# Attention with queries on partitions: scores once, the two maps of a differential head mixed into one, weights turned by TensorE transposes

## The chip, the cores and the metric

The kernel runs on one core of one Trainium2 chip. The core has a TensorE (PE in the profile; its weight loads are a row of their own, PEld), VectorE (DVE), ScalarE (ACT), GpSimd (POOL) and SyncE (SP, which here only issues DMAs). Each engine executes its instructions in the order in which they were built. The metric is the device time of one execution in microseconds; lower is better. All data are fp32. Matrices go through TensorE either as fp32, or as pairs (hi, lo) of fp32r numbers whose sum is the fp32 number, in several passes.

## What is computed

Two layers of a backbone run for 128 prompt tokens and 512 sample tokens (with 2 columns of zeros between them, 642 columns). Each layer is a mixer (differential attention, grouped-query attention, an SSD scan, an S5 scan, one output projection) and a gated ConvFFN. The change is in the two attentions. Sample tokens see their own 512 keys and 128 cached ones, prompt tokens see the prompt's 128 keys alone:

```python
def diff_attention(q, k, v, lam):
    scale = A_HALF ** -0.5
    k1, k2 = k[..., :A_HALF], k[..., A_HALF:]
    def block(qb):
        s1 = jnp.einsum('bqhd,bkhd->bhqk', qb[..., :A_HALF], k1).astype(F32) * scale
        s2 = jnp.einsum('bqhd,bkhd->bhqk', qb[..., A_HALF:], k2).astype(F32) * scale
        p = jax.nn.softmax(s1, axis=-1) - lam * jax.nn.softmax(s2, axis=-1)
        return jnp.einsum('bhqk,bkhd->bqhd', p.astype(v.dtype), v)
...
def gqa_attention(q, k, v):
...
        s = jnp.einsum('bqkgd,bskd->bkgqs', qg, k).astype(F32) * scale
        p = jax.nn.softmax(s, axis=-1)
        o = jnp.einsum('bkgqs,bskd->bqkgd', p.astype(v.dtype), v)
```

There are four differential heads of 64 features (two maps of 32 features each) and four grouped-query heads of 64 features, each two of which share a key head. The differential output is then normed per head.

## The kernel before

**Stages.** In the mixer the queries and keys come from the input projection (`lin3`: three passes over hi and lo parts, PSUM banks `psp`), are normed and rotated in `qk_prep`, split into hi and lo, and stored to DRAM as bands (`d_aq`, `d_ak`, `d_bq`, `d_bk`), from which attention loads them in the layout it wants. The S5 scan goes first; SSD, attention, the rest of the projections and, in layer 0, adaLN's products for later (`wm`, `sc`) then share the engines. A scheduler fixes the order of each engine when the kernel is built, by priorities (`PR`: S5 0, SSD 30000, attention 35000, projections 40000, the filling adaLN products 60000; the lower goes first among what is ready in its own model) and by the buffers that are free. SP issues all loads in one order as well.

**PSUM.** Eight banks: two for big tiles or `psp`, two of `e`, one each of `v` and `u`, two of `d`; `pss` (L157) hands them out. `e` and `u` serve attention's scores, `v` its output, `d` the SSD.

**Attention.** `attention` (L1314) runs six units: for each key half the differential heads' first maps, their second maps, and a grouped-query pair. A unit is two score maps, and `attn_unit` (L1119) gives it four parts. `load` brings cached keys (`ck`, L1135 or L1162), queries and keys (L1142 to L1171). `maxs` computes the scores with queries on the partitions (128 queries by 512 keys in bank `e`), takes row maxima on DVE (L1191; cached keys L1196), and turns them by small matmuls into a row that stands as an extra feature of the queries, with a row of ones on the keys' side (L1212). `probs` computes the scores again with keys on the partitions, the maximum now subtracted by that extra feature, exponentiates on ACT (`at_e`, L1237) and multiplies the values by these: weights of 64 columns (one head's values) and 512 moving columns (queries), in fp32 (`psv<-at_e,vt`). The exponentials are added over the key tiles on DVE and POOL (`at_s`, L1243), summed by a matmul with ones, and inverted by a reciprocal over 512 columns (L1254). `tail` divides, subtracts the second map's result from the first's, norms the head and splits the result for the output projection. The parts of three successive units are woven: `maxs` of unit u+1, `probs` of u, `tail` of u-1.

## Time and profile before

| | |
|---|---|
| device time, median of three runs | 2274.74 us (2268.22 to 2276.24) |
| span of the profiled execution | 2270.7 us |
| mean granted TensorE clock in it | 0.930 of full |
| PE busy | 2064.1 us (91%) |
| DVE, ACT, POOL busy | 1166.1, 728.5, 706.0 us |
| instructions | 32188 |

Busy times are sums of instruction lengths where they don't overlap; an engine at 91% over the whole span may still stand idle in a stage. The chain that ended last is followed back from the last instruction, each step to what released it. Windows give the same sums for stretches, with the granted clock as a share of full speed. Names are `out<-in`; L12 is line 12 of the kernel. A matmul's length overlaps the next one's, so what one holds of the engine is read from start to start.

### The profile page before, as it was taken

What the parts mean: (1) busy time and instruction counts of PE and PEld (TensorE: products, weight loads), DVE (VectorE), ACT (ScalarE), POOL (GpSimd) and SP (SyncE); (2) the same over time, 40 slices, a digit from 0 to 9 for tenths busy, and PEclk for the clock granted to TensorE, in tenths of its full rate; (3) what the DMA queues carried; (4) which work ended last, traced back from release to release, by engine and by line L of the source; (5) the groups of instructions that cost most, each with busy time, mean ns of one, the idle gap of its engine ahead of it and who ended that gap; (6) DMA issues with size and microseconds to landing.
All of it is one profiled execution on the core that took longest, in us unless ns stands there. A gap on an engine that the chain in (4) does not pass through costs nothing.

```text
span 2270.7 us, 32188 instructions
## 1 busy us (share of the span) xinstructions
PE 2064.1 (91%) x12698; PEld 1692.5 (75%) x12698; DVE 1166.1 (51%) x2376; ACT 728.5 (32%) x1256; POOL 706.0 (31%) x747
## 2 busy tenths in 40 slices
PE   5994988899999999999988889887989999999997
PEld 2884753454779788899976877655557899999985
DVE  7864874434558567233335358564565451323343
ACT  3421342232344223223324224343234443323231
POOL 4642523222232344122223324322233231212131
PEclk9996988889999999999998989888988999999998
DMA  7554324314313575422222542321022012222221
GB/s 285 165 179 135 121 68 124 93 49 142 108 38 108 166 247 186 131 82 63 84 77 77 174 131 90 111 67 49 11 65 94 19 47 84 70 80 68 82 75 47
DMA packets 95199, 232.19 MB, mean 102 GB/s; under 512 B 18120, under 2 KB 31816, under 8 KB 95048
## 3 DMA queue, kind: packets, MB, share of 16 engines
q1 hardware_dynamic: 95048, 230.14, 32.0%
q8 instruction: 100, 1.64, 0.3%
q14 instruction: 51, 0.42, 0.1%
HBM read 193.52 MB, written 36.58 MB: 101 GB/s over the span
## 4 chain that ended last, share of the span: by engine, by line
PE 75%; DMA 9%; DVE 7%; POOL 3%; issue 2%; ACT 2%; SPq 2%; POOLq 0%; DVEq 0%; ACTq 0%
PE psb L85 34%; PE psp L85 14%; PE pse L85 9%; PE psv L85 7%; PE psd L85 7%; PE psu L85 2%; DMA wm<-in_w_mod 1%; DMA ck<-in_cache_bk 1%; DMA ck<-in_cache_ak 1%; DMA wr<-in_w_down 1%; DMA s5yd<-s_u 1%; DMA wr<-in_w_out 1%; DMA s_tb<-s5td 1%; DMA s_u<-s5ud 1%; SPq L1160 1%
## 5 line engine op out<-in xcount | busy, mean ns | idle before, releaser
L85 PE MATMUL psb<-hh,wh 128*128 128x256 f32 (+1 forms) x1152 | 358.9, 312 | 2.3 <-DVE cv L425 2.3
L85 PE MATMUL psb<-hl,wh 128*128 128x256 f32 (+1 forms) x1152 | 357.9, 311 | 0.0
L85 PE MATMUL psb<-hh,wl 128*128 128x256 f32 (+1 forms) x1152 | 357.0, 310 | 0.0
L106 POOL TENSOR_TENSOR wl<-wr,wh 128x1024 fp32r<-128x1024 f32 (+3 forms) x83 | 181.6, 2188 | 449.5 <-ACT wh L103 427.1
L103 ACT CAST wh<-wr 128x1024 fp32r<-128x1024 f32 (+3 forms) x166 | 160.4, 966 | 427.9 <-PE psb L85 285.1
L85 PEld LDWEIGHTS psb<-hh,wh 128*128 128x128 f32 x1152 | 217.8, 189 | 13.2 <-issue 8.2
L85 PEld LDWEIGHTS psb<-hl,wh 128*128 128x128 f32 x1152 | 218.5, 190 | 3.4 <-issue 3.4
L85 PEld LDWEIGHTS psb<-hh,wl 128*128 128x128 f32 x1152 | 217.8, 189 | 3.4 <-issue 3.4
L85 PE MATMUL psp<-hh,wh 128*128 128x386 f32 (+1 forms) x544 | 182.2, 335 | 40.2 <-DVE dtr L839 13.1
L106 DVE TENSOR_TENSOR wl<-wr,wh 128x1024 fp32r<-128x1024 f32 (+3 forms) x83 | 95.2, 1147 | 184.5 <-ACT wh L103 184.0
L85 PE MATMUL psp<-hl,wh 128*128 128x386 f32 (+1 forms) x544 | 176.3, 324 | 1.5 <-DVE hl L353 1.4
L85 PE MATMUL psp<-hh,wl 128*128 128x256 f32 (+1 forms) x544 | 175.6, 324 | 0.0
L85 PE MATMUL psb<-uh,wh 128*128 128x256 f32 (+1 forms) x544 | 169.7, 312 | 0.0
L85 PE MATMUL psb<-ul,wh 128*128 128x256 f32 (+1 forms) x544 | 168.9, 310 | 0.0
L85 PE MATMUL psb<-uh,wl 128*128 128x256 f32 (+1 forms) x544 | 168.6, 310 | 0.0
L85 PEld LDWEIGHTS psp<-hh,wh 128*128 128x128 f32 x544 | 109.7, 202 | 52.8 <-DVE dtr L839 13.6
L85 PE MATMUL psv<-at_e,vt 128*64 128x512 f32 x240 | 136.3, 681 | 10.2 <-ACT at_e L1237 10.1
L1377 POOL TENSOR_TENSOR cv<-cv,cv 128x642 f32<-128x642 f32 x44 | 71.3, 1622 | 169.6 <-DVE cv L425 140.2
L85 PE MATMUL pse<-k,q 96*128 96x128 f32 (+5 forms) x288 | 100.2, 407 | 21.9 <-issue 6.7
L424 DVE SCALAR_TENSOR_TENSOR cv<-psb,vec,cv 128x641 f32<-128x641 f32 x72 | 63.4, 881 | 103.3 <-ACT cv L423 103.3
L85 PEld LDWEIGHTS pse<-k,q 96*128 96x128 f32 (+2 forms) x288 | 54.4, 205 | 79.0 <-issue 59.6
L85 PEld LDWEIGHTS psp<-hl,wh 128*128 128x128 f32 x544 | 109.5, 201 | 4.0 <-DVE hl L353 2.5
(497 smaller groups left out, 4596.5 us busy)
## 6 DMA issues: line engine op xcount, KB each, us to landing
wm<-in_w_mod SPq DMA_DIRECT2D x96, 512.0 KB
wr<-in_w_up SPq DMA_DIRECT2D x88, 512.0 KB
wr<-in_w_in SPq DMA_DIRECT2D x30, 512.0 KB
wr<-in_w_down SPq DMA_DIRECT2D x32, 384.0 KB
wr<-in_w_down SPq DMA_DIRECT2D x32, 320.0 KB
wr<-in_w_out SPq DMA_DIRECT2D x16, 512.0 KB
s_tb<-s5td SPq DMA_DIRECT2D x8, 992.0 KB
s_to<-s5td SPq DMA_DIRECT2D x8, 768.0 KB
```

Of the source, the lines that this page charges most:

```text
L85: self.nc.tensor.matmul(out, w, x, start=start, stop=stop)
L103: nc.scalar.copy(hv, rv)
L106: e.tensor_sub(lv, rv, hv.bitcast(F32))
L424: nc.vector.scalar_tensor_tensor(out[:, 1:TW], x[:, 0:TW - 1], w[:, 0:1], out[:, 1:TW], op0=ALU.mult, op1=ALU.add)
L1160: nc.sync.dma_start(k2[0:64, 0:TW].bitcast(F32), self.qd["bk"][0, r])
L1377: G.tensor_mul(cv[0], cv[0], cv[1])
```

## The change

Queries now stay on the partitions all the way. A unit of kind 0 is one differential head with both its maps; a unit of kind 1 is a pair of grouped-query heads as before. A unit is a list of items, the prompt and four tiles of 128 queries for each head, each with a `front` and a `back`; with `LAG = 1` the front of an item comes before the back of the one ahead of it.

`front` computes the scores of 128 queries with 512 keys into a bank of `e` (those of the cached keys for several tiles into `u`), takes the maximum on DVE, combines it with that of the cached keys and scales it in a small DVE step (L1252), and exponentiates on ACT with this as a bias for each partition; ACT sums the row as it goes (`accum_out`). For a differential head, `mix` adds the second map, times -lam and the ratio of the two sums, to the first: one operation on 128x640. `back` turns the weights by transposes on TensorE, four tiles of 128x128 into a bank of `e` (L1184), splits them into hi (ACT) and lo (DVE, L163), and multiplies: the turned weights are now the stationary operand, the values (as hi and lo side by side, `vhl`) move, 128 columns for hi and 64 for lo. The output has queries on its partitions, so division and head norm take a number for each partition; last it is turned back (L1293). The loads of a unit are issued before the items of the unit ahead of it, from two `k` buffers and four `q` buffers (before three and six), with `d_bk` as three bands and `d_bq` as two.

```diff
-KB = 3
+KB = 2
-QN = 6
-DEL = (4, 0, 0)
-STEP = (1, 1, 1)
-RSP = 1
+QN = 4
+LAG = 1
+NP = 4
-AB = ("e", "u", "e", "e", "u", "ue")
...
         lo = pool.tile([P, TW], F32R, tag="qk_lo", name="qk_lo")
         self.split(hi, lo, R)
-        n = 2 if name == "bk" else 3
+        n = 2 if name[:2] == "bq" else 3
...
-    def attn_unit(self, l, pool, kq, kind, u, aa=0):
+    def attn_unit(self, l, pool, kq, kind, u, m0=0):
...
+        if kind == 0:
+            c, hi = cached(256)
+            cv, hv = (t.rearrange("p (m k) -> p m k", m=2) for t in (c, hi))
+            nc.sync.dma_start(cv[0:96], self.a["cache_ak"][l, u, :, 2 * m0:2 * m0 + 2, :])
+            A.copy(kt_[0:64, :, CK], cv[0:64])
+            A.copy(hv[64:96], cv[64:96])
+            V.tensor_sub(kt_[64:96, :, CK], cv[64:96], hv[64:96].bitcast(F32))
+            for i in range(2):
+                f = 32 * (2 * m0 + i)
+                nc.sync.dma_start(q[i][0:96].bitcast(F32), self.qd[f"aq{u}"][:, f:f + 32])
+                nc.sync.dma_start(kt_[0:96, i, 0:TW].bitcast(F32), self.qd[f"ak{u}"][:, f:f + 32])
+            def score(out, i, qs, ks):
+                self.mm(out, q[i][0:96, qs], kt_[0:96, i, ks], True, True)
+        else:
+            k1, k2 = kt_[:, 0, :], kt_[:, 1, :]
+            r = slice(64 * u, 64 * u + 64)
+            nc.sync.dma_start(k1[:, 0:TW].bitcast(F32), self.qd["bk"][0:2, r])
+            nc.sync.dma_start(k2[0:64, 0:TW].bitcast(F32), self.qd["bk"][2, r])
+            c, _ = cached(128)
+            nc.sync.dma_start(c, self.a["cache_bk"][l, u])
+            A.copy(k1[:, CK], c)
+            V.tensor_sub(k2[0:64, CK], c[0:64], k1[0:64, CK].bitcast(F32))
+            for i in range(2):
+                r = slice(64 * i, 64 * i + 64)
+                nc.sync.dma_start(q[i].bitcast(F32), self.qd[f"bq{u}"][0:2, r])
+            def score(out, i, qs, ks):
+                self.mm(out, q[i][:, qs], k1[:, ks], True, False)
+                self.mm(out, q[i][0:64, qs], k2[0:64, ks], False, True)
+        vhl = kq.tile([P, 6, 128], F32R, tag="v", name="v", bufs=2)
+        c = 64 * (2 * u + m0 if kind == 0 else 4 + u)
+        v = self.vt[:, :, c:c + 64]
+        A.copy(vhl[:, :, 0:64], v)
+        G.tensor_sub(vhl[:, :, 64:128], v, vhl[:, :, 0:64].bitcast(F32))
+        def probs(i, ps, nb, p, z):
+            A.activation(p, ps, AF.Exp, bias=nb, scale=scale, accum_out=z)
+        def mix(p1, p2, z, rz):
+            t = z[:, 2:4]
+            V.reciprocal(t, z[:, 0:2])
+            V.tensor_copy(rz, t[:, 0:1])
+            V.scalar_tensor_tensor(t[:, 1:2], z[:, 0:1], self.nlam, t[:, 1:2], op0=ALU.mult, op1=ALU.mult)
+            V.scalar_tensor_tensor(p1, p2, t[:, 1:2], p1, op0=ALU.mult, op1=ALU.add)
+        def turned(srcs, ps):
+            n = 128 * len(srcs)
+            for j, s in enumerate(srcs):
+                nc.tensor.transpose(ps[:, 128 * j:128 * j + 128], s, self.c("ident"))
+            eh, el = (pool.tile([P, 512], F32R, tag=t, name=t, bufs=2)[:, 0:n] for t in ("at_h", "at_l"))
+            self.split(eh, el, ps[:, 0:n])
+            return [(eh[:, 128 * j:128 * j + 128], el[:, 128 * j:128 * j + 128]) for j in range(len(srcs))]
+        def values(o, e, kt, first, last):
+            self.mm(o, e[0], vhl[:, kt, :], first, False)
+            self.mm(o[:, 0:64], e[1], vhl[:, kt, 0:64], False, last)
+        def put(O, ps):
+            n = ps.shape[-1] // 128
+            o = ps.rearrange("p (t x d) -> p t x d", t=n, x=2)
+            A.copy(O, o[:, :, 0, :])
+            V.tensor_add(O, O, o[:, :, 1, :])
+        heads = (m0,) if kind == 0 else (0, 1)
+        rz, O, st = {}, {}, {}
+        def small():
+            return pool.tile([P, 16], F32, tag="at_s", name="at_s", bufs=4)
+        def prompt_front():
+            for m in heads:
+                rz[m] = pool.tile([P, 5], F32, tag="at_rz", name="at_rz", bufs=3)
+            ps = self.pss("e")
+            for i in range(2):
+                score(ps[:, 128 * i:128 * i + 128], i, PQ, PQ)
+            s = small()
+            V.reduce_max(s[:, 0:2], ps[:, 0:256].rearrange("p (m k) -> p m k", m=2), axis=AX.X)
+            V.tensor_scalar(s[:, 2:4], s[:, 0:2], -scale, None, op0=ALU.mult)
...
+        def front(m, qt):
+            maps = (0, 1) if kind == 0 else (m,)
+            j = qt % 2 * 2 if kind == 0 else qt
+            if j == 0:
+                cs = st["cs"] = self.pss("u")
+                jobs = [(t, i) for t in (qt, qt + 1) for i in maps] if kind == 0 else [(t, m) for t in range(4)]
+                for n, (t, i) in enumerate(jobs):
+                    score(cs[:, 128 * n:128 * n + 128], i, slice(128 * t, 128 * t + 128), CK)
+                mc = st["mc"] = pool.tile([P, 4], F32, tag="at_m", name="at_m", bufs=2)
+                V.reduce_max(mc, cs.rearrange("p (q k) -> p q k", q=4), axis=AX.X)
+            cs, mc = st["cs"], st["mc"]
+            s = small()
+            ps_, n = [], len(maps)
+            for k, i in enumerate(maps):
+                ps = self.pss("e")
+                score(ps, i, slice(128 * qt, 128 * qt + 128), slice(0, 512))
+                V.reduce_max(s[:, k:k + 1], ps, axis=AX.X)
+                V.tensor_scalar(s[:, 2 + k:3 + k], s[:, k:k + 1], mc[:, j + k:j + k + 1], -scale, op0=ALU.max, op1=ALU.mult)
+                p = pool.tile([P, 640], F32, tag="at_p", name="at_p", bufs=NP)
+                probs(i, ps, s[:, 2 + k:3 + k], p[:, 0:512], s[:, 4 + k:5 + k])
+                probs(i, cs[:, 128 * (j + k):128 * (j + k) + 128], s[:, 2 + k:3 + k], p[:, 512:640], s[:, 6 + k:7 + k])
+                ps_.append(p)
+            z = s[:, 8:12]
+            V.tensor_add(z[:, 0:n], s[:, 4:4 + n], s[:, 6:6 + n])
+            if kind == 0:
+                mix(ps_[0], ps_[1], z, rz[m][:, qt:qt + 1])
+            else:
+                V.reciprocal(rz[m][:, qt:qt + 1], z[:, 0:1])
+            st[m, qt] = ps_[0]
+        def back(m, qt):
+            if qt == 0:
+                st["out"], st["todo"] = self.pss("v"), []
+            p, todo, out = st[m, qt], st["todo"], st["out"]
+            todo += [(qt, kt, p[:, 128 * kt:128 * kt + 128]) for kt in range(5)]
+            while len(todo) >= 4:
+                group = todo[:4]
+                del todo[:4]
+                for (t, kt, _), e in zip(group, turned([g[2] for g in group], self.pss("e"))):
+                    values(out[:, 128 * t:128 * t + 128], e, kt if kt < 4 else 5, kt == 0, kt == 4)
+            if qt < 3:
+                return
+            o = O[m]
+            put(o[:, 0:4, :], out)
+            V.tensor_mul(o, o, rz[m].unsqueeze(2).to_broadcast([P, 5, 64]))
+            if kind == 0:
...
+            if m == 0:
+                return
+            for ts in ((0, 1, 2, 3), (4,)):
+                ps = self.pss("e")
+                n = 128 * len(ts)
+                for k, t in enumerate(ts):
+                    nc.tensor.transpose(ps[:, 128 * k:128 * k + 128], self.oo[:, t, :], self.c("ident"))
+                hi, lo = (t[:, CH[ts[0]]:CH[ts[0]] + n] for t in self.h[2 * u + kind])
+                if kind == 0:
+                    A.activation(hi, ps[:, 0:n], AF.Identity, scale=self.subg)
+                    V.scalar_tensor_tensor(lo, ps[:, 0:n], self.subg, hi.bitcast(F32), op0=ALU.mult, op1=ALU.subtract)
+                else:
+                    self.split(hi, lo, ps[:, 0:n])
+        return [(prompt_front, prompt_back)] + [(partial(front, m, qt), partial(back, m, qt)) for m in heads for qt in range(4)]
...
     def attention(self, l, pool, kq):
         self.attn_begin(l, pool)
-        stages = []
-        for unit in ((0, 0, 0), (0, 0, 1), (1, 0), (0, 1, 0), (0, 1, 1), (1, 1), None, None):
...
+        units = ((0, 0, 0), (0, 0, 1), (1, 0), (0, 1, 0), (0, 1, 1), (1, 1))
+        waiting, new = [], self.attn_unit(l, pool, kq, *units[0])
+        for i in range(len(units)):
+            items, new = new, self.attn_unit(l, pool, kq, *units[i + 1]) if i + 1 < len(units) else None
+            for front, back in items:
+                front()
+                waiting.append(back)
+                if len(waiting) > LAG:
+                    waiting.pop(0)()
+        for back in waiting:
+            back()
```

The bodies that the diff replaces are in the kernel above. In counts for both layers, gone are 120 products `psv<-at_e,vt`, 24 sums with ones of 512 columns, 160 matmuls of the second scores with 512 columns and some 200 smaller matmuls; new are 376 transposes and 672 value matmuls.

On PE, at the last unit of layer 0, before (`hh`, `hl` and `wh`, `wl` are the parts of activations and weights in a projection; `q,k` with `k` last are scores with keys on the partitions):

```order
L85 MATMUL psu<-q,k 128x512 x2
L85 MATMUL psv<-at_e,vt 64x512
L85 MATMUL pse<-q,k 128x512 x2
L85 MATMUL psp<-hh_72,wh 128x256
L85 MATMUL psp<-hl_73,wh 128x256
L85 MATMUL psp<-hh_72,wl 128x256
```

and now (`identr` is the identity that turns, `kh` weights of the output projection):

```order
L1184 MATMUL pse<-identr,at_p 128x128 x4
L84 MATMUL pse<-k,q 128x512 x2
L84 MATMUL psv<-v,at_h 128x128
L84 MATMUL psv<-v,at_l 128x64
...
L1293 MATMUL pse<-identr,at_o 128x128 x5
L84 MATMUL psp<-hh_84,kh 128x256 x2
```

Before, the input projections stood between the scores and values of this unit. Now the projections are done by then, and transposes, scores and values follow each other alone until the turned output.

On SP in layer 0, before, the loads of the third unit and the next (`ck` cached keys; `sd_h` belongs to the SSD):

```order
L1170 DMA q<-d_bq_2142 128x1x642
L1162 DMA ck<-in_cache_bk 128x128
L1171 DMA q<-d_bq_2142 64x642
L1143 DMA k<-d_ak_2464 96x1x642 x2
L952 DMA sd_h_3176<-in_ssd_h 128x256
L1142 DMA q<-d_aq_2448 96x1x642 x2
```

and now, from the second unit's cached keys on:

```order
L1135 DMA ck<-in_cache_ak 96x256
...
L1152 DMA ck<-in_cache_bk 128x128
...
L1157 DMA q<-d_bq_2143 128x1x642
...
L1149 DMA k<-d_bk 128x1x642
L1150 DMA k<-d_bk 64x642
L1157 DMA q<-d_bq_2143 128x1x642
```

The third unit's cached keys stood between its two loads of queries; they now come ahead of its queries and keys.

On DVE, in layer 0, before (`sd_` names are the SSD's):

```order
L1191 TENSOR_REDUCE mx<-pse 128x1 x2
L1243 TENSOR_TENSOR at_s<-at_s,at_e 128x512
L1024 TENSOR_TENSOR sd_ea<-sd_ea,psd 128x256
L1196 TENSOR_REDUCE mc<-pse 128x4
L1201 TENSOR_TENSOR mr<-mx,mc 128x2x4
```

and now:

```order
L1252 TENSOR_SCALAR at_s<-at_s,at_m 128x1
L163 TENSOR_TENSOR at_l<-pse,at_h 128x512
L968 SCALAR_TENSOR_TENSOR sd_h<-sd_h_3175,sd_small,psd 128x64 x2
L1258 TENSOR_TENSOR at_s<-at_s 128x2
...
L1175 RECIPROCAL at_s<-at_s 128x2
L1176 COPY at_rz<-at_s 128x1
L1177 SCALAR_TENSOR_TENSOR at_s<-at_s,lm_n 128x1
L1178 SCALAR_TENSOR_TENSOR at_p<-at_p,at_s 128x640
```

Row maxima and running sums of exponentials stood there before. A differential tile now comes to DVE for its maxima and the step of one column (L1252), again for the sum, the reciprocal, two more small steps and the mix over 640 columns (L1258 to L1178), and a third time for the low parts of its turned weights (L163).

## Rows read from the trace of the kernel before

**Rows 1.** page, parts 1 and 4: busy time and the chain by engine

```profile
PE 2064.1 (91%) x12698; PEld 1692.5 (75%) x12698; DVE 1166.1 (51%) x2376; ACT 728.5 (32%) x1256; POOL 706.0 (31%) x747
PE 75%; DMA 9%; DVE 7%; POOL 3%; issue 2%; ACT 2%; SPq 2%; POOLq 0%; DVEq 0%; ACTq 0%
```

**Rows 2.** windows: busy us of PE, PEld, DVE, ACT, POOL, clock, DMA, GB/s

```profile
190.00:300.00 110.00, 83.77 (x531) 68.69 (x531) 68.85 (x123) 32.45 (x56) 39.15 (x43) 0.81 0.41 128
...
500.00:590.00 90.00, 85.73 (x419) 44.04 (x420) 49.55 (x77) 27.72 (x51) 24.85 (x20) 0.96 0.47 147
...
sum 774.00, PE 669.73 PEld 430.57 DVE 434.42 ACT 240.22 POOL 242.61; mean PE 83.72 PEld 53.82 DVE 54.30 ACT 30.03 POOL 30.33
```

**Rows 3.** row maxima of layer 0 by line: ns min/median/max, first and last start

```profile
L1191 DVE TENSOR_REDUCE mx<-pse x48: 660/690/693, 189.8 to 526.1; 128x1 f32<-128x512 f32 x48
```

**Rows 4.** groups by line: busy us, mean ns of one, idle before

```profile
L85 PE MATMUL psv<-at_e,vt 128*64 128x512 f32 x240 | 136.3, 681 | 10.2 <-ACT at_e L1237 10.1
L85 PE MATMUL pse<-at_s,cst 128*64 128x512 f32 x48 | 26.3, 654 | 0.0
L85 PE MATMUL pse<-q,k 97*128 97x512 f32 (+3 forms) x112 | 41.3, 429 | 0.0
```

**Rows 5.** timeline, four stretches: start us, length us, engine, line, operation

```profile
262.09 1.07 PE L85 MATMUL psv<-at_e,vt 128*64 128x512 f32 x2
263.09 0.50 PE L85 MATMUL pse<-k,q 96*128 96x512 f32 x1
...
264.38 0.68 DVE L1191 TENSOR_REDUCE mx<-pse 128x1 f32<-128x512 f32 x1
...
270.67 0.34 PE L85 MATMUL psp<-hh,wh 128*128 128x386 f32 x1
270.85 0.34 PE L85 MATMUL psp<-hl,wh 128*128 128x386 f32 x1
...
335.44 0.71 PE L940 MATMUL psd<-identr,cf 128*128 128x128 f32 x5
335.91 0.90 PE L85 MATMUL pse<-k,q 128*128 128x512 f32 x2
...
1505.48 1.08 PE L85 MATMUL psv<-at_e,vt 128*64 128x512 f32 x4
...
1636.99 1.16 PE L85 MATMUL psd<-cst,sd_md 128*128 128x128 f32 x8
1638.08 1.07 PE L85 MATMUL psv<-at_e,vt 128*64 128x512 f32 x2
```

**Rows 6.** chain in order of time: start us, length us, what it waited for

```profile
301.14 9.09 DMA ck<-in_cache_bk
...
472.19 9.07 DMA ck<-in_cache_bk
...
1482.57 6.03 DMA ck<-in_cache_ak
...
1532.50 15.35 DMA ck<-in_cache_ak
...
1592.93 9.07 DMA ck<-in_cache_bk
```

**Rows 7.** groups by line and shape, DVE and ACT

```profile
L1254 DVE RECIPROCAL at_rec<-pse 128x512 f32<-128x512 f32 x12 | 40.3, 3356 | 14.5 <-PE pse L85 14.5
...
L1243 DVE TENSOR_TENSOR at_s<-at_s,at_e 128x512 f32<-128x512 f32 x36 | 36.7, 1021 | 17.9 <-ACT at_e L1237 17.9
...
L424 DVE SCALAR_TENSOR_TENSOR cv<-psb,vec,cv 128x641 f32<-128x641 f32 x72 | 63.4, 881 | 103.3 <-ACT cv L423 103.3
...
L1527 DVE TENSOR_TENSOR y<-y,psp 128x386 f32<-128x386 f32 x24 | 13.2, 552 | 21.1 <-PE psp L85 21.0
...
L1237 ACT ACTIVATE at_e<-pse 128x512 f32<-128x512 f32 x60 | 35.8, 596 | 98.2 <-PE pse L85 97.9
```

**Rows 8.** groups by line and shape, weight loads

```profile
L85 PEld LDWEIGHTS psd<-cst,sd_md 128*128 128x128 f32 x160 | 21.4, 205 | 8.4 <-ACT sd_ex L997 5.4 <-issue 2.2 <-DVE cf L1030 0.2
```

More of the change, by code (lines that the diff above doesn't have):

```diff
@@ L3 @@
 from contextlib import ExitStack, contextmanager
+from functools import partial
 import numpy as np
@@ L1296, in attn_unit @@
-        return load, maxs, probs, tail
+            r = slice(64 * u, 64 * u + 64)
[8 more added lines that the diff above has]
+                nc.sync.dma_start(q[i].bitcast(F32), self.qd[f"bq{u}"][0:2, r])
@@ new lines, in prompt_front @@
+        def prompt_front():
[7 more added lines that the diff above has]
+            V.tensor_scalar(s[:, 2:4], s[:, 0:2], -scale, None, op0=ALU.mult)
+            pp = pool.tile([P, 640], F32, tag="at_p", name="at_pp", bufs=NP)[:, 0:256].rearrange("p (m k) -> p m k", m=2)
+            for i in range(2):
+                probs(i, ps[:, 128 * i:128 * i + 128], s[:, 2 + i:3 + i], pp[:, i, :], s[:, 4 + i:5 + i])
+            if kind == 0:
+                mix(pp[:, 0, :], pp[:, 1, :], s[:, 4:8], rz[m0][:, 4:5])
+            else:
+                for m in heads:
+                    V.reciprocal(rz[m][:, 4:5], s[:, 4 + m:5 + m])
+            st["pp"] = pp
```

178 lines of the change are left out of this document (18 added, 160 removed).

## The prediction

> **What bounds the kernel now.** I read the busy shares first, then the chain that ended last, then the two attention stages by themselves, then single spacings on TensorE. TensorE matmuls cover 91% of the span, and the chain lies on PE for 75% of it, on DMA for 9% and on DVE for 7% [rows 1]. So the place to look is PE, but only where the change acts: the stage from the first row maximum of a layer (189.8 us in layer 0 [rows 3]) to the last output copy, which the windows 190 to 590 and 1316 to 1690 cover. There the sum over both layers is 774 us, with PE busy for 669.73, PE weight loads 430.57, DVE 434.42, ACT 240.22 and POOL 242.61 [rows 2]. Attention shares PE in this stage with the projections, the SSD and adaLN, which fill what attention leaves. Some 104 us of the 774 are idle on PE, and the granted clock is 0.81 at the start of layer 0 and 0.96 at its end, so part of the work runs at the lower of its two levels (1.2 and 2.4 GHz) [rows 2]. PE is the bound here, with gaps. Five of the gaps stand in the chain by name: the wait for cached keys, 9.09, 9.07, 6.03, 15.35 and 9.07 us, in sum 48.6 [rows 6].
>
> **What goes from PE.** Counts are of both layers; prices are from start to start, since a row's length also holds the drain of its last matmul.
> - Values on the exponentials: 120 products of 512 columns in fp32 (240 records [rows 4]). One that stands alone holds PE from 262.09 to 263.09, 1.00 us; four records, that is two products side by side, take 1.08 at 1505.48 [rows 5]. All alone 120 us, all paired 60; the busy time is 136.3 [rows 4]. I take 120, as most stand between other work.
> - Sums of the exponentials by a matrix of ones: 24 products of the same form (48 records, 26.3 busy [rows 4]): 24, at least 12.
> - The second computation of the scores. Before, each map's scores are made query-major for the maxima and again key-major for the exponentials. 160 matmuls of 512 columns go. A projection matmul of 386 columns comes every 0.18 us (270.67 to 270.85 [rows 5]), so 0.24 for 512; the mean length of the removed rows is 429 ns [rows 4], which their drain makes too large. At 0.35: 56 (38 to 69).
> - Some 200 small ones (maxima as an extra row, head norms, the prompt's sums): about 0.1 each, 20 (14 to 28).
> Together **220 us** (124 to 241).
>
> **What comes to PE.** 376 transposes of 128x128 in fp32: five in front of 335.91 take 0.47, so 0.094 each, more where other work stands between; at 0.11 it is 41 (35, and 79 at half clock) [rows 5]. 672 value matmuls with the turned weights as stationary side, each with a weight load of its own and 128 or 64 columns. The nearest row is `sd_md`, 8 matmuls with own weights of 128 columns between 1636.99 and 1638.08, 0.136 each [rows 5]; half of ours have 64 columns, so I take 0.12: 81 (47 if the 64-column ones cost a quarter and nothing stalls, 183 if all run at half clock). Together **122 us** (82 to 262). Net **−98**. The best ends together give −159. The bad ends belong to clocks and pairs that exclude each other in part: all old products paired and the new ones cheap gives −42, everything at half clock +21, which the granted 0.81 to 0.96 [rows 2] excludes as a mean.
>
> A rule speaks against this. The trace shows PE weight loads at 430.57 of 774 [rows 2], 205 ns each for `sd_md` [rows 8], and eight of these matmuls with their loads in 1.09 [rows 5]: the loads lie beside the matmuls. The Trainium skill, page "Perfetto Trace Analysis", section "Identifying the Most-Contended Engine", says that weight-load busy time, and not matmul busy time, tells how near TensorE is to its bound. By that rule the change loads TensorE more, since it adds 1048 loads and takes some 700; what it would give is a rival below.
>
> **Beside PE.** DVE loses 12 reciprocals of 512 columns at 3.36 us (40.3) and half of the running sums (36.7 in 36 of them [rows 7], which with the first ones is about 48). It gains 80 subtractions for the low parts: the nearest is an add of 386 columns out of PSUM at 552 ns [rows 7], so about 0.68 for 512, 54 us; 32 mixes of 640 columns at about 0.88, the row of the convolution's step [rows 7], 28; and some 300 operations of a few columns at about 0.15, 45. DVE goes up by about 20 in both layers together, from 56% of the stage to some 67% of a shorter one. The 96 maxima stay (0.69 each [rows 3]). ACT trades 120 exponentials at 0.60 [rows 7] for 96 of 512 and 96 of 128 columns and 80 casts: about +40, to some 40%. POOL loses its half of the sums. None of these comes near 100%, so I cost them at nothing as totals; what hides them is the projections and the SSD on PE, and where that cover ends they appear as hops (below).
>
> **Loads.** A unit's queries, keys and cached keys are now issued a unit ahead of its work, and the order on SP has `ck<-in_cache_bk` before the third unit's queries rather than between them. Two k buffers and four q buffers allow one unit ahead and no more; SP is also held by waits of other loads, which stand in front in layer 0 for the last unit. I take half of the 48.6 us [rows 6]: **−24** (0 to −48.6).
>
> **New chain.** A score tile now goes PE, DVE maximum, DVE small step, ACT exponential, DVE mix, PE transpose, ACT cast, DVE low part, PE values: seven hops to other engines, where before an exponential went straight into the values. One hop is seen: a score ends at 263.59 and its maximum starts at 264.38, 0.79 later [rows 5]. While projections and SSD lie between, PE does not wait. At the end of the stage they run out: about 12 of the 36 items of a layer stand alone on PE in the new order. An item there needs about 3 banks of two, each held about 3 us (score 0.35, hop 0.79, maximum 0.69, small step 0.15, exponential 0.60, another hop), some 4 us, and has about 2 us of PE work. 12 items, 2 us, two layers, and a little for the half done: **+24** (0 to +60). Before has this too, in a smaller measure, so this is an estimate from above rather than from the middle.
>
> **Sum.** −98 − 24 + 24 = −98. The profiled execution has a span of 2270.7; 4.0 lie around it to the median of 2274.74. 2274.7 − 98 gives **2177 us**.
>
> **Rivals.**
> A. Larger gain. If the stage keeps its idle share (PE at 670 of 774 [rows 2]), −98 of work is −113 of time, and with all cached-key waits gone and no cost at the tail the change is worth −162: 2113. For it: the idle time before is made of waits for the same banks and buffers that now serve fewer products. Against it: the longer chain. Chance 0.22, with all between 2090 and 2135.
> B. The hops eat most of it. DVE visits each tile three times (maximum, mix or reciprocal, low part) behind the SSD's long operations in an engine that runs in order; half a microsecond more of PE wait at each of the 176 score tiles and transpose groups gives back 88: 2265. The weight loads as the bound belong here. If a transpose or a value matmul cost its weight load, 0.15 to 0.205 [rows 8], and not 0.11 and 0.12, the 1048 would be 194 and not 122, +72: 2249. Against it: the eight in 1.09. Beside it stands the rule of the section "Identifying the Most-Contended Engine" in the Trainium skill's page "Perfetto Trace Analysis", which points to this case. Chance 0.19 in all, of which 0.08 is no change (within 0.5%, 11 us, about what a measurement of this kernel can tell).
> C. Slower: the ring of two PSUM banks `e`. All score tiles, all transpose groups, the prompt and the turned outputs go through these two: 48 + 40 + 14 + 8 = 110 uses in a layer. A stage of 387 us (half of 774) is kept if a bank is held for 7.0 us on the mean; my shortened stage of 338 allows 6.1. The bare hold is about 3. If DVE and ACT, in order and shared with the SSD, stretch it to 7.5, a layer takes 412, and the kernel 50 us more than now: 2325. For it: the hold now includes both DVE and ACT in turn, before only one of them. Against it: twice the bare hold still fits. Chance 0.14.
>
> **How the numbers follow.** The forecast, 2177, with all between 2135 and 2235, has 0.45. A has 0.22, B 0.19, C 0.14. Faster by over 0.5%: 0.45 + 0.22 + 0.11 = 0.78; within: 0.08; slower: 0.14. The range goes from 2095, a little under A, to 2265, B's end; it leaves out C and the far end of A, about 0.18 together.
>
> **What would show it.** Right: PE busy in the two stages falls from 670 to about 570; the stages shorten by about 49 us each; the values and sums in fp32 are gone from the list, `psv<-v,at_h` and `at_l` come every 0.12; the rows for `ck` in the chain are fewer than five; gaps on PE grow only at the end of a stage, with DVE or ACT as releaser. A shows no such gaps. B shows DVE as the releaser all over the stage, or value matmuls at 0.2. C shows PE idle before `pse` for DVE `at_l` or ACT `at_p`, with holds of a bank over 7 us. The forecast is wrong if fewer products stood alone than I take (removal 160, not 220), if the new small matmuls run mainly at half clock, or if work other than attention is pushed behind the stage, so that the next stage pays.

## The result, and the profile after

The change made the kernel **slower by 1.1%**: 2301.59 us, median of four runs (2297.77 to 2311.28), against 2275.49 (2268.22 to 2280.07). The ratio is 1.0113, with a 95% interval of 1.0077 to 1.015. The forecast was 2177, in a range of 2095 to 2265; the time lies outside it and on the other side of no change.

The page of the changed kernel, parts 1 and 4:

```profile
PE 2056.9 (90%) x12990; PEld 1806.6 (79%) x12990; DVE 1196.2 (52%) x2784; ACT 796.0 (35%) x1608; POOL 648.3 (28%) x695
PE 67%; DVE 9%; DMA 8%; ACT 3%; issue 1%; POOL 1%; SPq 1%; POOLq 0%; ACTq 0%; DVEq 0%
```

Against [rows 1], PE is busy for 7 us less, not 98. The shares of this chain add up to only 90%, since it could be followed back no further than to 209.6 us; so 75% and 67% can't be compared as they stand. Over the stretch that both chains cover, from 213 us to the end, PE has 79% before and 74% now, DVE 6% and 10%, ACT 2% and 3%. The same windows as [rows 2], here in two pieces, of the kernel before:

```profile
190.00:590.00 400.00, 338.22 (x1710) 201.65 (x1711) 213.03 (x387) 118.94 (x232) 117.81 (x124) 0.85 0.35 107
1316.00:1690.00 374.00, 331.51 (x1851) 228.93 (x1850) 221.38 (x411) 121.28 (x240) 124.80 (x138) 0.89 0.23 71
```

and of the changed kernel, with the end of each attention stage by itself:

```profile
190.00:590.00 400.00, 309.30 (x1803) 240.38 (x1803) 221.84 (x575) 145.49 (x388) 92.94 (x103) 0.76 0.34 106
1316.00:1690.00 374.00, 324.73 (x2044) 285.76 (x2043) 247.60 (x611) 155.28 (x399) 111.90 (x127) 0.77 0.28 91
...
540.00:612.00 72.00, 60.83 (x210) 46.96 (x210) 27.23 (x70) 21.59 (x63) 2.61 (x3) 0.50 0.00 0
1630.00:1720.00 90.00, 74.27 (x255) 55.74 (x253) 43.59 (x105) 35.02 (x93) 11.28 (x8) 0.50 0.16 54
```

PE does less in the same stretch, and at a lower clock: 0.76 and 0.77 on the mean after 0.85 and 0.89. Over 72 us at the end of layer 0's stage and 90 near the end of layer 1's the granted clock is 0.50, the lower level, though PE is busy for 84% and 83% of them. In 500 to 590 of the kernel before it was 0.96 [rows 2].

**The account of PE.** I worked it out from the starts of PE's matmuls: each is given the time to the next one's start, at most its own length, and what is left over is idle. Over the whole execution, in us:

| | before | after | forecast of the difference |
|---|---|---|---|
| attention's matmuls | 306.9 | 286.7 (−20) | −98 |
| all other matmuls | 1756.6 | 1769.7 (+13) | 0 |
| idle on PE | 176.9 | 211.6 (+35) | 0 (loads −24, hops +24) |
| sum (some 30 us lie ahead of the first matmul and behind the last) | 2240.4 | 2268.0 (+28) | −98 |

The sum's +28 is the loss: the spans differ by 27.3. Nearly all arises by the end of layer 0's mixer: the first matmul of its ConvFFN (`psb`) starts at 733.9 instead of 710.7, layer 1's at 1849.4 instead of 1822.1.

### The profile page after: what moved, and what is told of

The parts are those of the page before. It is cut to its first block, busy times and chain, and to the rows that moved or that the text cites. A ratio compares the mean times of both kernels' runs of the same rounds, so it can differ in the third digit from the quotient of the medians.

```text
span 2298.0 us, 33434 instructions
## 1 busy us (share of the span) xinstructions
PE 2056.9 (90%) x12990; PEld 1806.6 (79%) x12990; DVE 1196.2 (52%) x2784; ACT 796.0 (35%) x1608; POOL 648.3 (28%) x695
## 4 chain that ended last, share of the span: by engine, by line
PE 67%; DVE 9%; DMA 8%; ACT 3%; issue 1%; POOL 1%; SPq 1%; POOLq 0%; ACTq 0%; DVEq 0%
PE psb L84 33%; PE psp L84 11%; PE pse L84 7%; PE psd L84 7%; PE psv L84 6%; DMA wm<-in_w_mod 2%; PE pse L1184 2%; PE psu L84 1%; DMA wr<-in_w_down 1%; DMA wr<-in_w_out 1%; ACT at_p L1170 1%; DMA d_bq<-qk_lo 1%; DMA wr<-in_w_up 1%; DMA s_tb<-s5td 1%; DVE kl L105 1%
## 5 line engine op out<-in xcount | busy, mean ns | idle before, releaser
L84 PEld LDWEIGHTS psb<-hl,wh 128*128 128x128 f32 x1152 | 218.5, 190 | 4.2 <-issue 4.2
L84 PE MATMUL psp<-hl,wh 128*128 128x386 f32 (+1 forms) x544 | 180.9, 333 | 1.8 <-DVE hl L352 1.8
L301 POOL TENSOR_TENSOR rq_y<-rq_x,cst 128x2 f32<-128x2 f32 (+3 forms) x34 | 39.1, 1150 | 358.8 <-DVE rq_x L299 342.2
L84 PE MATMUL psv<-v,at_h 128*128 128x128 f32 x320 | 110.1, 376 | 22.3 <-ACT at_h L162 22.3
L84 PEld LDWEIGHTS psp<-hh,wl 128*128 128x128 f32 x544 | 112.5, 207 | 2.1 <-issue 1.0
```

The lines of the kernel that those rows point to most:

```text
L84: self.nc.tensor.matmul(out, w, x, start=start, stop=stop)
L301: self.nc.gpsimd.tensor_tensor(y, x, self.c("mhalf")[:, 0:n], op=ALU.pow)
```

## The experiments

Ratios are to the kernel before, run on the same chips (medians 2277.9 to 2280.7; it was 2275.5 beside the changed kernel), with 95% intervals. Every variant gets an order of its own from the scheduler: layer 0's ConvFFN starts 17.6 us sooner in `no_sub` than in the changed kernel, though both take the same time in the end. So differences under some 10 us between variants carry little.

### The low parts, and which half of them

All low parts left out:

```diff
-            self.mm(o, e[0], vhl[:, kt, :], first, False)
-            self.mm(o[:, 0:64], e[1], vhl[:, kt, 0:64], False, last)
+            self.mm(o, e[0], vhl[:, kt, :], first, last)
...
-            self.split(eh, el, ps[:, 0:n])
+            A.copy(eh, ps[:, 0:n])
```

> The changed kernel without the low parts of the turned weights: 336 value matmuls of 64 columns and 96 DVE subtractions are left out, and the output loses accuracy. If PE bounds the stage (theory A): 336 times 0.08 to 0.17 us, 27 to 57 us faster than the changed kernel, near or under the kernel before. If the hops bound it (theory C): the hop through DVE goes for 88 groups, at about 1 us each where not covered, 10 to 25 us faster.

2252.19 us, 0.9889 (0.9859 to 0.992): −49 against the changed kernel. This takes away both a hop through DVE and 336 matmuls. Two runs part them. `no_sub` has only the second hunk, and gives the high part in place of the low one to the second matmul:

> The changed kernel with the DVE subtractions for the low parts left out (96), but all 336 value matmuls of 64 columns kept: they take the high part a second time, so the output is not the right one. PE's work is as in the changed kernel. If the hop through DVE is what the split costs: 30 to 50 us faster than the changed kernel (2302 us), as far as without low parts (2252) or with fp32 values (2257). If the extra matmuls are what it costs: within 12 us of the changed kernel.

2300.64 us, 1.0096 (1.0077 to 1.0116), no difference from the changed kernel. `sub_only` has only the first hunk, so the subtractions stay:

> The changed kernel with the 96 DVE subtractions kept and the 336 value matmuls of 64 columns left out; the low parts are made and read by nobody. The hop no longer stands between turning and values, but a bank of e is still held until DVE has read it, and DVE has the same work. If the wait of the values for DVE is the cost: 30 to 50 us faster than the changed kernel. If it is the bank and DVE's time: within 15 us of it. If it is PE's work: 27 to 57 us faster, and no_sub is not.

2254.88 us, 0.9899 (0.9877 to 0.9922): the whole gain. PE's account in it: attention 231.1 (−55.6), idle 218.5 (+7). So the second matmul of each pair costs it, 46.7 us for 336, 0.14 each, and the hop through DVE is worth nothing by itself: what it made PE wait, PE waits elsewhere (idle is 219.9 in `no_sub`, 211.6 in the changed kernel). Their two prices are seen on either side of the clock's fall. The changed kernel's PE timeline (start, length, operation):

```profile
492.48 0.60 PE L1184 MATMUL pse<-identr,at_p 128*128 128x128 f32 x4
492.84 0.31 PE L84 MATMUL psv<-v,at_h 128*128 128x128 f32 x1
492.98 0.25 PE L84 MATMUL psv<-v,at_l 128*128 128x64 f32 x1
493.06 0.31 PE L84 MATMUL psv<-v,at_h 128*128 128x128 f32 x1
...
590.58 0.47 PE L84 MATMUL psv<-v,at_h 128*128 128x128 f32 x1
590.86 0.36 PE L84 MATMUL psv<-v,at_l 128*128 128x64 f32 x1
591.03 0.45 PE L84 MATMUL psv<-v,at_h 128*128 128x128 f32 x1
591.28 0.36 PE L84 MATMUL psv<-v,at_l 128*128 128x64 f32 x1
...
592.31 1.11 PE L1184 MATMUL pse<-identr,at_p 128*128 128x128 f32 x4
593.08 1.50 PE L84 MATMUL pse<-k,q 128*128 128x512 f32 x2
594.50 0.47 PE L84 MATMUL psv<-v,at_h 128*128 128x128 f32 x1
```

Beside projections at 492 a pair takes 0.14 + 0.08 and a transpose 0.09. Alone at 591 a pair takes 0.25 + 0.17, a transpose 0.19, a score matmul 0.71. From 590.58 to 594.50 goes one group of four turned tiles with a score: PE works without a gap and still needs 3.9 us for it; by the spacings at 492 the four pairs and four transposes alone would take 1.2 and not 2.5.

### Can the clock be lifted?

First by more work on PE: two fp32r matmuls of 512 columns, of no use, for each query tile of the last unit, into a bank of the projections.

```diff
+            for _ in range(DUMMY if (u, kind) == (1, 1) else 0):
+                self.mm(self.pss("p"), self.identr, kt_[:, 0, 0:512], True, True)
```

> The changed kernel with two extra fp32r matmuls of 512 columns in front of each of the eight query tiles of the last unit of a layer (32 in all), whose result nobody reads. Theory A (PE at the lower clock bounds the end of the stage, and more streaming work lifts the clock): the clock in the last unit rises from 0.50, an item goes from 4.1 us to 3 us or less, and the kernel gets 10 to 20 us faster although it does more. Theory B (clock stays low): 32 times 0.43 us, 14 us slower. Theory C (hops bound it): no change, the extra work fits into gaps.

2297.43 us, 1.0116 (1.0058 to 1.0174), with the widest spread of all (2287.91 to 2316.13). It also moved the projections, so it settles little; in the last unit of layer 1 the windows stay at 0.50 (1680 to 1720). The next two put such matmuls ahead of the score into its own bank, four for each score of the last unit (64 in all), or one for each of the 96 scores:

```diff
+                for _ in range(4 if (u, kind) == (1, 1) else 0):
+                    self.mm(ps, self.identr[0:r], kt_[0:r, 0, 0:512], True, True)
                 score(ps, i, slice(128 * qt, 128 * qt + 128), slice(0, 512))
```

> The changed kernel with four extra fp32r matmuls of 512 columns ahead of each score in the last unit of a layer, into the bank that the score then overwrites; 64 in all, read by nobody, and the order of the rest stays nearly as it is. In the changed kernel an item there takes about 4.1 us at a granted clock of 0.50. Theory A (the clock sets the pace of the end, and small matmuls leave it low): the clock goes up in the last unit, an item takes 2.4 us for its own work and 0.9 for the extra one, the kernel gets 5 to 15 us faster although it does 64 matmuls more. Theory B (the clock stays at 0.50 there for another reason): 64 times 0.43, 25 to 30 us slower. Theory C (hops between engines): 0 to 15 us slower, since the extra work fills gaps in part.

> The changed kernel with one extra fp32r matmul of 512 columns ahead of each of the 96 scores of 512 keys, in the bank that the score overwrites. Theory A: the mean clock rises above 0.887, and the 20 to 40 us of extra work are paid back in part or in full: within 15 us of the changed kernel. Theory B: the clock stays, 96 times 0.22 to 0.43, 20 to 40 us slower.

2323.28 us (1.0174, 1.0134 to 1.0215) and 2311.4 us (1.0131, 1.0102 to 1.0161). In the windows of the first, at the end of layer 0, PE is full and the clock stays low:

```profile
580.00:600.00 20.00, 19.75 (x72) 15.01 (x72) 7.15 (x17) 5.73 (x16) 0.00 (x0) 0.59 0.00 0
600.00:620.00 20.00, 19.54 (x65) 14.59 (x64) 7.37 (x18) 5.89 (x17) 0.00 (x0) 0.50 0.00 1
```

At the end of layer 1 the same matmuls do lift it in part. Its last unit stands nearly alone on PE from 1697 to 1754, and the windows show 0.64 and 0.66:

```profile
1700.00:1720.00 20.00, 17.10 (x58) 11.45 (x57) 6.81 (x20) 5.59 (x19) 0.00 (x0) 0.64 0.06 25
1720.00:1740.00 20.00, 19.19 (x74) 14.37 (x73) 8.06 (x19) 5.50 (x18) 0.00 (x0) 0.66 0.00 1
```

In the changed kernel, where the last unit stands so from 1677 to 1729, they show 0.50:

```profile
1680.00:1700.00 20.00, 17.96 (x54) 12.15 (x53) 8.09 (x24) 7.02 (x23) 0.00 (x0) 0.50 0.00 1
1700.00:1720.00 20.00, 19.50 (x73) 15.64 (x73) 9.03 (x24) 8.29 (x23) 0.00 (x0) 0.50 0.00 0
```

The kernel loses 21.7 us all the same, 0.34 for each of the 64. One for each score (`fill1_all`) came out as its theory A has it: the granted clock of its four runs is 0.894 to 0.895, after 0.886 to 0.889, and the 96 hold PE for 37.6 us in the account but cost 9.8. The ends of both its stages stay at 0.50, so the clock rose elsewhere. The rest of attention takes 14 us less in it and idle is 4 us less; how much of this is the clock and how much the order was not parted. More matmuls between thus lifted the clock in places and in neither form paid for themselves. Then by the form of the turning: a plain fp32 matmul with the identity in place of the transpose, which takes two records instead of one.

```diff
-                nc.tensor.transpose(ps[:, 128 * j:128 * j + 128], s, self.c("ident"))
+                self.mm(ps[:, 128 * j:128 * j + 128], s, self.c("ident"), True, True)
```

> The changed kernel with one line changed: the weights are turned by an ordinary fp32 matmul with the identity, not by a transpose. In the changed kernel attention stands alone on PE at 540 to 612 us and 1640 to 1720 us with a granted clock of 0.50 and PE busy up to 10.00 of 10; a transpose then takes 0.21 us from start to start against 0.11 elsewhere. Theory A (the end of the stage is bound by PE at the lower clock, and transposes are what keeps it there): the clock rises in these two stretches, and the kernel stays within 10 us of the changed one or gets faster although each turning costs twice as much. Theory B (the clock stays low whatever the form of the turning): 336 turnings cost 0.1 to 0.25 us more each, 35 to 80 us slower than the changed kernel, about 2340 to 2380. Theory C (the hops between engines bound the end, not PE): nearly no change, within 10 us, and the clock at 0.50 as before.

2309.03 us, 1.0137 (1.0088 to 1.0185). The time is the changed kernel's within the spread, but the inside is another: the granted clock of the profiled run is 0.908 against 0.887, and in 600 to 620, where the changed kernel has 0.54, the windows show

```profile
600.00:620.00 20.00, 18.28 (x97) 15.76 (x96) 8.47 (x20) 6.48 (x18) 0.00 (x0) 0.74 0.00 1
```

PE's account: turning 118.0 (+52), but values 97.0 (−14), scores 94.8 (−9), idle 193.4 (−18). The clock is higher in all its runs (0.899 to 0.911, against 0.886 to 0.889); whether by the form of the turning or by the 52 us of added work was not parted. The form costs as much as it gives back.

### The order, and the depth of the chain

Attention ahead of everything in the scheduler's priorities:

```diff
-PR = {"proj": 40000, "s5": 0, "glu": 10000, "ssd": 30000, "attn": 35000, "f0": 60000, "f1": 61000, "tab": 50000, "st": 55000, "lead": 299000, "wg": 165000, "norm": 300000, "first": 310000}
+PR = {"proj": 40000, "s5": 0, "glu": 10000, "ssd": 30000, "attn": 25000, "f0": 60000, "f1": 61000, "tab": 50000, "st": 55000, "lead": 299000, "wg": 165000, "norm": 300000, "first": 310000}
```

> The changed kernel with attention's priority set ahead of the SSD's (25000 against 30000), so that SSD work and not attention alone stands at the end of the stage. Theory A: the stretch at 0.50 shrinks, PE's mean clock rises above 0.887, 15 to 30 us faster than the changed kernel. Theory C: the chain of hops gets longer cover, too, and gains 10 to 20, with the clock no better. If the cause is neither (loads that come late in layer 0, about 15 us of PE idle at 497 to 511), nothing changes.

2327.04 us, 1.022 (1.0188 to 1.0251). Idle on PE rises from 211.6 to 227.2. Too low a priority of attention is not what costs the time; which work then waits longer was not followed up.

A front two items ahead of its back, with buffers for it, without and with low parts. With them something else shrinks to make room: the low parts' buffers, or the values'. Each such run has a control that shrinks the same and keeps the lag. LAG = 2 with all buffers kept was not run.

```diff
-LAG = 1
-NP = 4
+LAG = 2
+NP = 5
```

> The changed kernel without the low parts, and with the front of an item two items ahead of the back of the one before (LAG 2, five weight buffers, in the room that the low parts leave), so that more independent work stands between the hops. Theory C (hops between engines bound the end of the stage): 10 to 25 us faster than without low parts alone (2252 us). Theory A (PE at the lower clock): within 8 us.

> The changed kernel, complete, with the front of an item two items ahead of the back (LAG 2, five weight buffers); the room comes from one buffer for the low parts and three for the small sums, so it is to be compared with l1. Hop theory (PE waits in its order for ACT's and DVE's steps between score and values: 52 us of such waits at 250 to 590 us and 33 at 1340 to 1700 in the changed kernel's trace): 15 to 40 us faster than l1. Clock theory alone (the small matmuls at 0.50 set the time, whatever their order): within 8 us of l1.

> The changed kernel with one buffer for the low parts of the turned weights (two before) and three for the small sums (four before): the control for lag2_l1. Hop theory: 0 to 15 us slower than the changed kernel, since one more wait is made. Clock theory: within 8 us.

> The changed kernel, complete, LAG 2 and five weight buffers, with both buffers for the low parts kept; the room comes from a single buffer for the split values. To be compared with v1. In lag2_l1 the low parts had one buffer and the second item of distance brought nothing. If that one buffer was what took the gain away: 15 to 40 us faster than v1. If the split itself takes it away (a bank of e is held by ACT's cast and then by DVE's subtraction, and DVE comes late), within 10 us of v1.

> The changed kernel with one buffer for the split values, not two: the control for lag2_v1. The values of the next unit then wait for the last product of the unit ahead: 0 to 15 us slower than the changed kernel.

| | lag 1 | lag 2 | idle on PE, lag 1 and 2 |
|---|---|---|---|
| no low parts | 2252.19 | 2215.33 (0.9708, 0.9679 to 0.9737) | 220.7, 195.7 |
| low parts, one buffer for `at_l` | 2308.27 (1.0123, 1.0104 to 1.0142) | 2312.66 (1.0148, 1.0132 to 1.0163) | 217.2, 207.0 |
| low parts, one buffer for `v` | 2304.16 (1.011, 1.0076 to 1.0144) | 2328.43 (1.0227, 1.0207 to 1.0248) | 214.0, 229.0 |

Where an item is cheap on PE the hops are what is left, and a second item in flight takes 37 us away (25 of idle, 13 of attention's matmuls). With the low parts the lag gives nothing or harms. Why it harms with one buffer for `v` isn't settled; that one buffer holds back the next unit once two items are open is a guess that no run parts from the new order.

### Values in fp32: a version that beats both

`no_lo` with the turning in one fp32r pass, too:

> The changed kernel without the low parts of the turned weights (336 value matmuls and 96 DVE subtractions left out), and with the weights kept in fp32r and turned by an ordinary fp32r matmul in one pass, not by an fp32 transpose: the weights are rounded to fp32r. Against the one without low parts alone (2252 us): theory A (PE and its clock): a turning costs 0.06 to 0.12 us and not 0.11 to 0.21, and the clock is better held: 15 to 40 us faster than that one. Theory C (hops): within 8 us of it, since no hop goes.

2244.22 us, 0.984 (0.9808 to 0.9871), 8 us less than `no_lo`. Turning takes no less of PE so (72.3 us in the account, against 68.6); the form of the pass is no way out.

The next keeps the whole computation and drops the split: the turned weights are copied once, in fp32, and one fp32 matmul of 64 columns (two records on PE) takes the place of the pair.

```diff
-            self.split(eh, el, ps[:, 0:n])
+            A.copy(eh, ps[:, 0:n])
...
-            self.mm(o, e[0], vhl[:, kt, :], first, False)
-            self.mm(o[:, 0:64], e[1], vhl[:, kt, 0:64], False, last)
+            self.mm(o[:, 0:64], e[0], v[:, kt, :], first, last)
```

> The changed kernel, complete, with the split undone: the turned weights are copied once, as fp32, and one fp32 matmul of 64 value columns takes the place of the two fp32r matmuls of 128 and 64 columns. On PE the two cost 0.22 us together at full clock and 0.43 at half; the fp32 one should be near 0.25 to 0.35 by its four-fold stream of 64 columns and its weight load, so PE is about even. DVE loses 96 subtractions and the hop through it goes. Hop theory: 20 to 45 us faster than the changed kernel. Clock and PE theory: within 12 us.

2257.1 us, 0.9911 (0.9895 to 0.9928). PE is about even, as expected: sorted by the granted clock at its start, a product takes 0.22 us at full clock and 0.44 at the lower level, and a pair in the changed kernel 0.23 and 0.47. What this frees of memory is enough for LAG = 2 (with NP = 6 and QN = 5):

> The same with the front two items ahead of the back, six weight buffers and five query buffers, in the room that the split values leave. Both causes are eased without any loss of accuracy. Hop theory: another 20 to 40 us, to some 2220 to 2245, faster than the kernel before. Clock and PE theory: within 8 us of fp32_values.

**2218.82 us, 0.9741 (0.9725 to 0.9758)**: 57 us under the kernel before and 83 under the change. Its groups by line:

```profile
L84 PE MATMUL psv<-vt,at_h 128*128 128x64 f32 x640 | 109.4, 327 | 1.7 <-ACT at_h L1183 1.7
...
L1181 PE MATMUL pse<-identr,at_p 128*128 128x128 f32 x320 | 64.6, 344 | 7.3 <-ACT at_p L1167 6.7 <-ACT at_o L1193 0.6
```

and those of the changed kernel that answer to them, with its other new groups:

```profile
L84 PE MATMUL psv<-v,at_h 128*128 128x128 f32 x320 | 110.1, 376 | 22.3 <-ACT at_h L162 22.3
L84 PE MATMUL psv<-v,at_l 128*128 128x64 f32 x320 | 95.9, 308 | 17.2 <-DVE at_l L163 17.0
L1184 PE MATMUL pse<-identr,at_p 128*128 128x128 f32 x320 | 68.9, 356 | 14.4 <-DVE at_p L1178 9.2 <-ACT at_p L1170 4.3 <-DVE at_o L1198 0.9
L163 DVE TENSOR_TENSOR at_l<-pse,at_h 128x512 fp32r<-128x512 f32 x80 | 54.7, 686 | 45.1 <-ACT at_h L162 44.8
L1178 DVE SCALAR_TENSOR_TENSOR at_p<-at_p,at_s 128x640 f32<-128x640 f32 x32 | 28.9, 904 | 0.3
L1170 ACT ACTIVATION_READ_ACCUMULATOR at_p<-psu,at_s 128x1 f32 x96 | 19.5, 203 | 0.0
L1170 ACT ACTIVATION_READ_ACCUMULATOR at_p<-pse,at_s 128x1 f32 x96 | 18.9, 197 | 0.0
```

PE's idle ahead of the value matmuls falls from 39.5 us (22.3 and 17.2) to 1.7. In the account attention is 257.1 (−30 against the change) and idle 171.4 (−40). Its clock at the end of layer 0's stage is no better, 0.50 from 540 to 580. The step from lag 1 to 2 is −38 here and was −37 without low parts, where there were four query buffers as before; what the fifth adds here was not parted. In part open is why the first step gives 45: the account of `fp32_values` has 24 less in attention, 10 less idle and 10 less in other work, and it also drops casts on ACT, subtractions on POOL and adds on DVE, which weren't parted. A lag of three (NP = 7, QN back to 4), and lag two with the turning by plain matmuls:

> Complete, values in one fp32 matmul, LAG 3, seven weight buffers and four query buffers. Hop theory: between 2200 and 2222, a little faster than LAG 2 if hops are still waited for, and the same if two items cover them. If the gain of LAG 2 came from the fifth query buffer and not from the distance: back to about 2245 or more.

> Complete, values in one fp32 matmul, LAG 2, and the weights turned by an ordinary fp32 matmul with the identity. Against fp32_values_lag2 (2219 us): its 336 turnings cost about 0.1 us more each at full clock, 35 us; if they hold the clock up at the end of the stage as turn_mm's did in part (mean clock 0.887 to 0.908), half or more of it comes back: 2220 to 2240. If the clock stays, 2255 or more.

2237.96 us (0.9832, 0.9808 to 0.9855) and 2242.89 us (0.9849, 0.9816 to 0.9882). The first falls between its two cases, so it doesn't settle what the fifth query buffer does; a third item in flight with four gains 19 us on `fp32_values` and not 38. The second has the highest clock of all variants, 0.926, and in it the clock comes up while attention still stands alone on PE, in layer 0 from 560.6 us on, after 20 us of the same work at 0.50. In the transposes' version it stays down to the end of that work. Its window, then that of `fp32_values_lag2`; attention is alone on PE until 579 and 577:

```profile
560.00:580.00 20.00, 18.19 (x134) 15.63 (x133) 5.26 (x15) 9.68 (x25) 0.00 (x0) 0.98 0.00 1
```

```profile
560.00:580.00 20.00, 18.55 (x81) 16.58 (x81) 5.02 (x14) 8.48 (x22) 0.00 (x0) 0.50 0.01 1
```

Even so turning costs 43 us more in the account (104.7 against 61.6), and values and other work give back 23.

## Why the prediction was wrong

**What goes: right.** Values on the exponentials 118.7 us (predicted 120), sums 22.8 (24), second scores 57.3 (56), small ones 22.7 (20). The sum is 221.5, predicted 220. The reading of prices from start to start [rows 5] held, with some luck in the first term: sorted by the granted clock at its start, a product took 0.88 us at full clock and 1.62 at the lower level, and only the mix gives the 1.00 that was read from one of them.

**What comes: the step that failed.** Predicted 122: 41 for transposes and 81 for values. Measured 182.7: 66.3 and 116.4. The count was right, and so were the prices at full clock: sorted in the same way, a transpose of the weights takes 0.11 us there, as predicted, and a pair in bank `v` 0.23 where 0.24 was taken. But half of both start at the lower level (162 of 320 transposes, 314 of 640 value matmuls), where they take 0.22 and 0.47. All of attention's PE time, sorted so, was 238 us at full clock and 69 at the lower level, and is now 98 and 189. At full clock the 189 would be about half, an estimate from these prices, and attention would be at some 190 us, near the 209 of the forecast (306.9 − 98). I set aside the bound at half clock because the granted clock of the stage was 0.81 to 0.96 [rows 2]. That was the clock of the kernel before, whose stage the change alters: I had written myself that a third of the items would stand alone on PE, and then priced them as if the projections still stood beside them.

**What stays: not costed.** The first scores with queries on the partitions are the same matmuls in both kernels and cost 85.4 us before and 104.1 after, +19; projections, SSD and the rest +13. These are the same instructions, and the clock is the difference that their rows show: of the 288 first scores 46 started at the lower level before and 137 do now, of the other matmuls 771 and 923. In attention, +35 and +25 on what comes and +19 on what stays turn −98 into −20.

**Hops: the direction right, the size not.** Predicted +24 at the end of the stage; its own terms, 12 items, 2 us and two layers, give 48, and no number in it takes half of that away. PE's waits over the whole run (engine, line, what it waited for; us, times, longest):

```profile
PE psv L84 <- ACT at_h L162: 22.3, 10, 15.1
PE pse L1184 <- ACT at_p L1170: 21.3, 7, 13.1
PE psv L84 <- DVE at_l L163: 17.0, 13, 5.6
...
PE pse L1293 <- POOL at_o L1286: 13.6, 2, 8.5
...
PE pse L1184 <- DVE at_p L1178: 9.2, 1, 9.2
```

These are 83 us, and not many short ones but few long ones. Attention's waits for ACT, DVE and POOL came to 18 us in the kernel before. The longest shows how one arises. ACT's timeline, and PE's behind it:

```profile
490.91 0.59 ACT L162 CAST at_h<-pse 128x512 fp32r<-128x512 f32 x1 [0.29 <-PE pse L1184]
509.53 1.04 ACT L102 CAST kh<-wr 128x1024 fp32r<-128x1024 f32 x1 [18.03 <-DMA wr<-in_w_out]
510.48 0.58 ACT L162 CAST at_h<-pse 128x512 fp32r<-128x512 f32 x1
```

```profile
511.11 0.47 PE L84 MATMUL psv<-v,at_h 128*128 128x128 f32 x1 [15.13 <-ACT at_h L162]
```

ACT runs in order and stands at the cast of an output-projection weight that DMA hasn't brought; attention's cast is queued behind it, and PE behind that. The weight's load was issued only at 496.46: from 479.87 on the chain stands on SP, first at the keys and queries of attention's next unit (L1150, L1157), then at loads of `x` (L1603). I costed DVE and ACT at nothing as totals; what counted was what stands in their queue ahead of a hop.

**Loads: the named waits went, the −24 did not come.** The five waits for `ck` [rows 6] have become one in the chain, and other loads have come in:

```profile
262.81 16.31 DMA d_bq<-qk_lo
...
482.32 6.01 SPq L1157
...
496.46 13.05 DMA wr<-in_w_out
...
1479.58 6.76 DMA ck<-in_cache_ak
```

DMA as a whole has 181 us before and 191 now of the stretch that both chains cover.

**Sizes beside PE: right.** The low part 0.69 us (0.68 predicted), the mix 0.90 (0.88). Not foreseen: an exponential that sums its row issues a second instruction on ACT of 0.20 us, some 38 us in the two groups above; ACT rose by 67.5 us where +40 was taken. For DVE the prediction says about +20, but its own terms (54, 28 and 45 come, 40 and 48 go) give +39; measured +30.

**Rivals.** A fell: idle rose. B's sign fits the longer chain, but its price for weight loads (of its 0.15 to 0.205 only the 0.205 stands in [rows 8]) does not: eight matmuls with their loads still follow each other at 0.08 to 0.14 at full clock. The rule of the Trainium skill named with it (page "Perfetto Trace Analysis", section "Identifying the Most-Contended Engine") pointed the right way, since weight-load busy time rose from 430.57 us to 526.14 in the same windows (240.38 and 285.76) while matmul busy time fell. The section asks for the share of the peak matmul rate beside it, which was not worked out here. As an explanation these runs don't bear it out: over the whole execution weight loads are busy for 1692.5 us (75%) before, 1806.6 (79%) now and 1783.1 (80%) in `fp32_values_lag2`, the fastest whole version. C was right in sign and wrong in mechanism. Worked out from the trace, a bank of `e` is held by a score for 6.1 us on the mean in layer 0 and 5.0 in layer 1, by a transpose group for 4.0 and 3.5; these means stay under the 7.0 from which C decides.

**The forecast's own signs.** It named "if the new small matmuls run mainly at half clock" as what would make it wrong, had a price for it (+21), and gave it no chance of its own. That was the second failure: it belonged among the rivals.

## What to carry to other kernels

Price added TensorE work at the clock that it will have in its new neighbourhood, not at the stage's clock before: work that fills the engine alone, in small matmuls and transposes, ran here at the lower level though the engine was busy for 83% and more of the stretch. When a change multiplies hops, look at what stands ahead of each hop in the in-order queue of its engine (here a cast waiting for a DMA), and try a second item in flight before judging the idea (it gave 37 and 38 us once the split pair of value matmuls was gone, and nothing with it). Where the turned data is the stationary side, one fp32 product cost no more on TensorE than a pair of split ones, and it freed the buffers that the second item needed.

## What the hardware showed that was not expected

- A stretch with PE busy for 19.54 to 19.75 of 20 us at a granted clock of 0.50 to 0.59 (`fill4_last`).
- Replacing fp32 transposes by plain fp32 matmuls with the identity raised the granted clock of the run from 0.887 to 0.908, and from 0.910 to 0.926 in the version with fp32 values; in one 20 us window, with nearly nothing but attention on PE, from 0.50 to 0.98. What in them does it was not parted further.
- A value matmul of 128 columns and one of 64, each with its own weights: 0.14 and 0.08 us at full clock, 0.25 and 0.17 at the lower level.
- `accum_out` on an exponential is an ACT instruction of its own, 0.20 us, whether it sums 512 columns or 128.
